# Feed-forward: sums of weight blocks by accumulating DMAs, and fifteen of twenty-two pairs in the seven-product scheme

## The chip, the cores and the metric

The kernel runs on one core of a Trainium2 chip. The metric is device time in microseconds (us) of one execution, the median of several runs; lower is better. The core's engines work side by side and wait for each other through semaphores: TensorE (PE, matrix products; PEld is its weight load), VectorE (DVE), ScalarE (ACT), GpSimd (POOL) and SyncE (SP, which here only issues loads). Sixteen DMA engines carry out the transfers that SP, ACT and POOL issue. Each engine takes its own instructions strictly in program order.

## The reference

The reference computes a two-layer encoder trunk on a sequence of 512 positions of width 1024, in float32. Each layer has a mixer (attention in the first, a chunkwise recurrent mLSTM in the second), a memory cross-attention and a gated convolutional feed-forward part, each behind an RMS norm. Only the feed-forward part is touched:

```python
def conv_ffn(xn, w_up, conv_w, conv_b, w_down):
    h = causal_depthwise_conv(xn @ w_up, conv_w) + conv_b      # w_up: 1024 x 5632
    g, u = jnp.split(h, 2, axis=-1)
    return (jax.nn.gelu(g) * u) @ w_down                       # w_down: 2816 x 1024
```

The width 2816 of `g` and `u` is 22 blocks of 128 columns. A "pair" p is block p of `g` together with block p of `u`; it needs two column blocks of `w_up`, p and 22 + p, each 1024 x 128.

## The kernel before

**Precision by splitting.** Every float32 operand is split in a high part (a cast on ACT) and a low part (a subtraction on DVE, L259), and a product is three matmuls: high by high, low by high, high by low (`mm3`, L268 to L270). Weights arrive as `raw` tiles and are split to `wh` and `wl`.

**A plain pair** (`plain`, L1282). For each of the two column blocks: one load of 512 KB, a split of 128x1024, and 8 x 3 matmuls with 512 columns moving (all positions). DVE then scales the result from PSUM to a tile `hs` (L1291).

**A seven-product pair** (`seven`, L1301). The pair's weights are seen as a 2 x 2 block matrix: row halves of 512 of the model width by the two column blocks, and the activations as 2 x 2 blocks by the same row halves and by halves of 256 positions. Seven block products instead of eight give the result (a scheme of the Strassen-Winograd kind). Each product is 4 x 3 matmuls with 256 columns moving, so the pair has 84 of them, half as wide as the 48 of a plain pair. The price is sums of blocks. With A11 and A12 the halves of `up[p]`, and A21 and A22 those of `up[22 + p]`, as they are stored, four sums are needed: S1 = A21 + A22, S2 = S1 + A11, S3 = A21 + A11, S4 = S2 + A12. Before, DVE makes them, each a TENSOR_TENSOR of 128x512 (`sum4`, L1329), in one tile `sum` with a single buffer; five splits follow (L1317 for the casts): `f3` of A11 and A12, `s2` of S2, `f1` of S1 and S3, `a22` of A22, `s4` of S4. The sums of activation blocks (`th`, `tl`) are made once per layer by `forms` (L1213). On the result side are five more DVE sums of 128x256 (L1372), one copy and one scaled copy on ACT, and a scaling of `hs` (L1393).

**The tail** of each pair (`tail`, L1237): two filter results on ACT, four filter taps on DVE (L1254), the GELU, the product, and the split of the activation `ah`, `al`.

**The down product** (`down`, L1403) works in chunks of four pairs (the last one of six): for each of eight output blocks a load of 256 KB, a split of 128x512, and 12 wide matmuls. These blocks are put between parts of later pairs: `plain` calls `fill` twice and `seven` three times, and each call takes one waiting down block. Eight are put on the list at pairs 5, 9, 13 and 18.

**What sets the order.** The feed-forward part is not written in its final order. Each step is a task with an engine, an estimated duration, what it depends on, a due time and the buffers it takes and frees; `Sched` (L139) plays all engines forward when the kernel is built and gives each engine a fixed order: whatever can start earliest, and of equals the one due first. Buffers are taken in the order in which the tasks were written. `load` (L1142, its DMA at L1145) is a task of SP. At most three `raw` tiles, three split weights of 128x1024 (`h`), two `hs` tiles and four PSUM accumulators are open at a time.

Before, the pairs 4, 6, 8, 10, 12, 14, 15, 17 and 19 of each layer use seven products. POOL does little: it clears two columns of each new `hs` tile (L1277).

## Time and profile before

| What | Value |
|---|---|
| median of 3 runs | 1513.41 us (1512.3 to 1513.85) |
| time of the profiled execution | 1512.78 us |
| its span, first to last instruction | 1511.0 us, 21313 instructions |
| granted TensorE clock, mean | 0.998 |
| first feed-forward part | about 416 to 774 us |
| second feed-forward part | about 1147 us to the end |
| HBM read and written | 143.04 MB and 2.10 MB, 96 GB/s over the span |
| DVE, low part of a 128x1024 weight (L259) | 197 times, 1222 ns |
| DVE, sums of weight blocks (L1329) | 72 times, 685 ns |
| ACT, high part of a 128x1024 weight (L262, L1159, L1317) | 1045 to 1051 ns |
| load of 512 KB / 256 KB / 384 KB, issue to landing | 3.3 / 2.6 / 3.0 us |

The span is one execution recorded by the profiler; the device time is a little longer than the span. Busy times are sums of records, so an engine's share is an average over stages with different limits. Matmuls and DVE operations are pipelined: the record of one runs on while the next has begun, so the distance between two starts is what an operation costs its engine, and the duration in a row is longer than that. "Idle before, releaser" names what an engine had waited for.

### The profile page before, as it was taken

Reading aid. Unit: us, or ns where it says so; the run is one execution under the profiler, and the core shown is the slowest. Engines: PE = TensorE matmul, PEld = TensorE weight load, DVE = VectorE, ACT = ScalarE, POOL = GpSimd, SP = SyncE. Lnnn points to the kernel's source line nnn. Section 1 sums busy time; section 2 is a strip of 40 time slices with the busy share of each in tenths; the row PEclk is TensorE's granted clock in tenths of the full one; section 3 lists DMA queues with packets and bytes.
Section 4 is the critical chain, followed back from the end, with each engine's and each line's share of the span. In section 5 each row is a group of like instructions: output and inputs, shape, how many; then the busy total and the mean of one; then the engine's idle time right before and its main releaser. Section 6 shows DMA issues by size and latency. Waiting matters only on the chain.

```text
span 1511.0 us, 21313 instructions
## 1 busy us (share of the span) xinstructions
PE 1500.0 (99%) x8026; PEld 1281.7 (85%) x8026; DVE 1160.1 (77%) x2155; ACT 774.8 (51%) x1282; POOL 44.0 (3%) x118
## 2 busy tenths in 40 slices
PE   9999999999999999999999999999999999999998
PEld 8888888888888888988888778888888888888887
DVE  7889885766699788897678857666557988889864
ACT  6768564444465444454446634444445554444444
POOL 2000120000000000000001100000000000000000
PEclk9999999999999999999999999999999999999999
DMA  5222233323223333232222222332323332333322
GB/s 179 84 71 84 84 103 108 112 96 100 95 101 100 97 108 109 84 112 88 81 90 84 80 89 93 99 101 99 111 84 109 108 94 95 98 103 106 102 60 77
DMA packets 47480, 146.52 MB, mean 97 GB/s; under 512 B 5649, under 2 KB 5649, under 8 KB 47377
## 3 DMA queue, kind: packets, MB, share of 16 engines
q1 hardware_dynamic: 46368, 144.04, 29.4%
q8 instruction: 63, 1.03, 0.3%
q10 hardware_dynamic: 1008, 1.12, 0.2%
q14 instruction: 41, 0.33, 0.1%
HBM read 143.04 MB, written 2.10 MB: 96 GB/s over the span
## 4 chain that ended last, share of the span: by engine, by line
PE 92%; DVE 3%; ACT 2%; issue 1%; DMA 1%; POOL 0%; SPq 0%; DVEq 0%; POOLq 0%; ACTq 0%
PE acc L268 19%; PE acc L269 19%; PE acc L270 19%; PE w L269 5%; PE w L268 5%; PE w L270 5%; PE acc L330 2%; PE acc L331 2%; PE acc L329 2%; PE s L268 2%; PE s L269 2%; PE s L270 2%; PE w L1595 1%; PE w L681 1%; PE s L395 1%
## 5 line engine op out<-in xcount | busy, mean ns | idle before, releaser
L268 PE MATMUL acc<-xh,wh 128*128 128x512 f32 (+1 forms) x944 | 356.9, 378 | 0.0
L270 PE MATMUL acc<-xh,wl 128*128 128x512 f32 (+1 forms) x944 | 352.8, 374 | 0.0
L269 PE MATMUL acc<-xl,wh 128*128 128x512 f32 (+1 forms) x944 | 352.6, 374 | 0.0
L259 DVE TENSOR_TENSOR wl<-raw,wh 128x1024 fp32r<-128x1024 f32 (+2 forms) x215 | 258.0, 1200 | 51.9 <-ACT wh L262 38.1
L262 ACT CAST wh<-raw 128x1024 fp32r<-128x1024 f32 (+2 forms) x137 | 140.9, 1030 | 168.5 <-PE acc L269 99.6
L270 PEld LDWEIGHTS acc<-xh,wl 128*128 128x128 f32 x944 | 177.5, 188 | 31.7
L268 PEld LDWEIGHTS acc<-xh,wh 128*128 128x128 f32 x944 | 177.6, 188 | 30.4
L269 PEld LDWEIGHTS acc<-xl,wh 128*128 128x128 f32 x944 | 177.7, 188 | 30.3
L1254 DVE SCALAR_TENSOR_TENSOR c<-hs,vec,c 128x512 f32<-128x512 f32 x176 | 128.4, 746 | 7.4 <-ACT c L1247 6.8
L269 PE MATMUL w<-al,wh 128*128 128x512 f32 x304 | 118.5, 390 | 0.0
L268 PE MATMUL w<-ah,wh 128*128 128x512 f32 x304 | 118.5, 390 | 0.0
L270 PE MATMUL w<-ah,wl 128*128 128x512 f32 x304 | 118.3, 389 | 0.0
L1159 ACT CAST wh<-raw 128x1024 fp32r<-128x1024 f32 (+1 forms) x60 | 61.3, 1022 | 77.8 <-PE acc L269 49.3
L1247 ACT ACTIVATE c<-hs,vec 128x512 f32<-128x512 f32 x88 | 70.0, 812 | 40.2 <-DVE hs L1393 23.5
L495 DVE TENSOR_TENSOR x<-w,x 128x512 f32<-128x512 f32 x72 | 49.5, 687 | 31.9 <-PE w L270 31.6
L270 PEld LDWEIGHTS w<-ah,wl 128*128 128x128 f32 x304 | 57.1, 188 | 12.0
L268 PEld LDWEIGHTS w<-ah,wh 128*128 128x128 f32 x304 | 57.1, 188 | 10.9
L269 PEld LDWEIGHTS w<-al,wh 128*128 128x128 f32 x304 | 57.1, 188 | 10.7
L1159 ACT CAST wh<-dr 128x512 fp32r<-128x512 f32 x64 | 39.7, 620 | 47.9 <-issue 17.4
L1268 ACT CAST ah<-c 128x512 fp32r<-128x512 f32 x44 | 27.3, 620 | 68.9 <-DVE c L1264 68.9
L330 PE MATMUL acc<-wl,xh 128*128 128x256 f32 (+1 forms) x192 | 61.9, 323 | 0.2 <-DVE wl L259 0.2
L329 PE MATMUL acc<-wh,xh 128*128 128x256 f32 (+1 forms) x192 | 61.7, 326 | 0.0
(373 smaller groups left out, 3323.4 us busy)
## 6 DMA issues: line engine op xcount, KB each, us to landing
raw<-in_up_dram SPq DMA_DIRECT2D x88, 512.0 KB, 3.3
dr<-in_down_dram SPq DMA_DIRECT2D x64, 256.0 KB, 2.6
raw<-in_xk_dram SPq DMA_DIRECT2D x16, 512.0 KB, 3.3
raw<-in_wo_dram SPq DMA_DIRECT2D x16, 512.0 KB, 3.2
raw<-in_xq_dram SPq DMA_DIRECT2D x16, 512.0 KB, 3.3
raw<-in_xv_dram SPq DMA_DIRECT2D x16, 512.0 KB, 3.3
raw<-in_xo_dram SPq DMA_DIRECT2D x16, 512.0 KB, 3.3
raw<-in_down_dram SPq DMA_DIRECT2D x16, 384.0 KB, 3.0
```

Of the source, the lines that this page charges most:

```text
L259: self.nc.vector.tensor_tensor(out=lo, in0=v, in1=hi.bitcast(F32), op=ALU.subtract)
L262: self.nc.scalar.copy(hi, v)
L268: mm(out, wh, xh, start=first, stop=False, skip_group_check=parts)
L269: mm(out, wh, xl, start=False, stop=False, skip_group_check=parts)
L270: mm(out, wl, xh, start=False, stop=last, skip_group_check=parts)
L329: mm(ps, xh[k][:, ts], wh[:, ws], start=(k == 0), stop=False)
L330: mm(ps, xh[k][:, ts], wl[:, ws], start=False, stop=False)
L331: mm(ps, xl[k][:, ts], wh[:, ws], start=False, stop=(k == 7))
L495: self.nc.vector.tensor_tensor(out=self.x[m][:], in0=ps[:], in1=self.x[m][:], op=ALU.add)
L1159: nc.scalar.copy(st["wh"][:, :cols], st[tag][:, :cols])
L1247: nc.scalar.activation(st["c_"][:, j, :], hs()[:, j, 2:514], AF.Identity, scale=self.col("cw", (layer * 3 + 2) * 44 + blk), bias=self.col( ...
L1254: nc.vector.scalar_tensor_tensor(out=c, in0=hs()[:, j, n : n + 512], scalar=w, in1=c, op0=ALU.mult, op1=ALU.add)
```

## The change

The change touches the feed-forward part of both layers.

- Pairs 4 to 15 and 17 to 19 of each layer use seven products: 15 instead of 9.
- The four DVE sums of a seven-product pair are gone. A tile `sa` is loaded with A11 and A21 side by side (a plain DMA on SP's queue); then an accumulating DMA, issued on POOL's queue, adds A21 and A22 from memory onto it, which leaves S3 and S1. A tile `sb` is loaded with A11, an accumulating DMA adds S1 from `sa` onto it, which leaves S2; after S2 has been split, a third accumulating DMA adds A12 from memory, which leaves S4. Each of them waits for the transfers before it.
- A11 and A12 are loaded once more as a whole for `f3` (`raw`), and A22 alone into a new tile `ra`. In all four plain loads and three accumulating ones per pair.
- The scheduler counts an accumulating DMA as 0.0029 us per column on POOL and 2.5 us until it has landed; a plain load as 0.0017 us per column and 2.0 us, as before.
- `hs` becomes two fixed tiles that POOL clears once per layer. `forms` uses the tile `sa`, of which there are two, in place of `sum`, of which there was one.
- The space that the program sets aside for the descriptors of POOL's DMAs (`dynamic_dma_scratch_size`) is given as 2048, where nothing was given before.

The diff, cut to its core:

```diff
--- before.py
+++ after.py
@@ -23,7 +23,7 @@
 NPAIR = DFF // P
 CHUNKS = [(0, 4), (4, 4), (8, 4), (12, 4), (16, 6)]
 
-SEVEN = (4, 6, 8, 10, 12, 14, 15, 17, 19)
+SEVEN = (4, 5, 6, 7, 8, 9, 10, 11, 12, 13, 14, 15, 17, 18, 19)
 EPS = 1e-6
 
 X_AT, X_STEP = 2.6, 0.6
@@ -1121,7 +1121,7 @@
 
 
         nc, t = self.nc, self.t
-        sc = Sched(raw=3, h=3, s2=1, s4=1, a22=1, sum=1, hs=2, c=1, dr=2, v=1, u2=1, u3=1, act=10, acc=4, s=2, w=2)
+        sc = Sched(raw=3, h=3, s2=1, s4=1, a22=1, sa=2, sb=2, ra=2, hs=2, c=1, dr=2, v=1, u2=1, u3=1, act=10, acc=4, s=2, w=2)
         add = sc.add
         tt = lambda n: 0.14 + 1.06e-3 * n
         act = lambda n: 0.2 + 0.83e-3 * n
@@ -1139,10 +1139,17 @@
         def joined(deps, prio, free):
             return add("-", 0.0, None, deps, prio, (), free, 0.0)
 
+        RAWS = {"raw": (self.wp, 1024, 3), "dr": (mp, 512, 2), "sa": (mp, 1024, 2), "sb": (mp, 512, 2), "ra": (mp, 512, 2)}
+
+        def raw_tile(st, tag):
+            pool, n, bufs = RAWS[tag]
+            st[tag] = self.til(pool, tag, (P, n), bufs=bufs)
+            return st[tag]
+
         def load(st, tag, src, cols, at):
             def fn():
-                st[tag] = self.til(*((self.wp, "raw", (P, 1024)) if tag == "raw" else (mp, tag, (P, 512))), bufs=3 if tag == "raw" else 2)
-                nc.sync.dma_start(st[tag][:, :cols], src)
+                to = raw_tile(st, tag)[:, :cols]
+                nc.sync.dma_start(to.rearrange("p (a b) -> p a b", a=2) if len(src.shape) == 3 else to, src)
 
             return add("SP", 0.0017 * cols, fn, (), at, [(tag, st)], (), 2.0)
 
@@ -1209,6 +1216,9 @@
         self.pad(mp, 192)
         th, tl = ([mp.tile([P, 1024], F32R, name=f"t{i}{layer}{k}", tag=f"t{i}{k}") for k in range(4)] for i in "hl")
         formed, pads = [], []
+        hs2 = [mp.tile([P, 2, 514], F32, name=f"hs{layer}{i}") for i in range(2)]
+        for h in hs2:
+            nc.gpsimd.memset(h[:, :, 0:2], 0.0)
 
         def forms(k, at):
 
@@ -1216,22 +1226,22 @@
 
             def scaled(j):
                 if j == 0:
-                    st["t"] = self.til(mp, "hs", (P, 2, 514))
+                    st["t"] = hs2[st["_hs"]][:, :, 2:514]
                 nc.scalar.activation(st["t"][:, j, :512], self.x[k + 4 * j][:], AF.Identity, scale=self.col("ffn", layer * 8 + k + 4 * j))
 
             def first():
-                st["r"] = self.til(mp, "sum", (P, 1536), bufs=1)[:, :1024]
+                st["r"] = raw_tile(st, "sa")[:]
                 tt_(out=pair(st["r"][:, :512]), in0=pair(st["t"][:, 0, :512]), in1=st["t"][:, :, 256:512], op=ALU.subtract)
 
             T1, T3, T2, T4 = (slice(256 * i, 256 * i + 256) for i in range(4))
             tt_ = nc.vector.tensor_tensor
             a = add("ACT", ACV, lambda: scaled(0), (), at, [("hs", st)])
             a = add("ACT", ACV, lambda: scaled(1), [a], at)
-            a = add("DVE", tt(512), first, [a], at, [("sum", st)])
+            a = add("DVE", tt(512), first, [a], at, [("sa", st)])
             a = add("DVE", tt(256), lambda: tt_(out=st["r"][:, T2], in0=st["t"][:, 1, 256:512], in1=st["r"][:, T1], op=ALU.add), [a], at)
             a = add("DVE", tt(256), lambda: tt_(out=st["r"][:, T4], in0=st["t"][:, 1, 0:256], in1=st["r"][:, T2], op=ALU.subtract), [a], at, (), [("hs", st)])
             h = add("ACT", act(1024), lambda: nc.scalar.copy(th[k][:], st["r"]), [a], at)
-            formed.append(add("DVE", tt(1024), lambda: self.sub(tl[k][:], st["r"], th[k][:]), [h], at, (), [("sum", st)]))
+            formed.append(add("DVE", tt(1024), lambda: self.sub(tl[k][:], st["r"], th[k][:]), [h], at, (), [("sa", st)]))
 
 
         def tail(p, st, deps, at):
@@ -1273,8 +1283,7 @@
 
         def rows(st, at):
             def fn():
-                st["hs_"] = self.til(mp, "hs", (P, 2, 514))
-                nc.gpsimd.memset(st["hs_"][:, :, 0:2], 0.0)
+                st["hs_"] = hs2[st["_hs"]]
 
             return add("-", 0.0, fn, (), at, [("hs", st)])
 
@@ -1299,12 +1308,23 @@
 
 
         def seven(p, fill):
-            st, r1, r2, f1, f3, s2, s4, a22 = ({} for _ in range(8))
+            st, sa, sb, r2, f1, f3, s2, s4, a22 = ({} for _ in range(9))
             at = clock[0]
-            l1 = load(r1, "raw", t["up"][layer, 22 + p], 1024, at - 16.0)
-            l2 = load(r2, "raw", t["up"][layer, p], 1024, at - 16.0)
-            A21, A22, A11, A12 = (lambda: r1["raw"][:, :512]), (lambda: r1["raw"][:, 512:]), (lambda: r2["raw"][:, :512]), (lambda: r2["raw"][:, 512:])
+            A1, A2 = t["up"][layer, p], t["up"][layer, 22 + p]
             tt_ = nc.vector.tensor_tensor
+            up2 = t["up"][layer].rearrange("(j p) r c -> p r j c", j=2)
+
+
+            def onto(out, src, cols, deps, due):
+                return add("POOL", 0.0029 * cols, lambda: nc.gpsimd.dma_start(out(), src(), accum_op=ALU.add), deps, due, (), (), 2.5)
+
+            SB = lambda: sb["sb"][:]
+            b1 = load(sa, "sa", up2[p][:, :, :512], 1024, at - 20.0)
+            b1 = onto(lambda: sa["sa"][:], lambda: A2, 1024, [b1], at - 16.0)
+            b2 = load(sb, "sb", A1[:, :512], 512, at - 18.0)
+            b2 = onto(SB, lambda: sa["sa"][:, 512:], 512, [b1, b2], at - 9.0)
+            l2 = load(r2, "raw", A1, 1024, at - 10.0)
+            l1 = load(a22, "ra", A2[:, 512:], 512, at - 6.0)
 
             def small(s, tag):
                 if tag == "s4" and not pads:
@@ -1319,27 +1339,13 @@
                 h = add("ACT", act(cols), hi, deps, due - 3.0, take)
                 return add("DVE", tt(cols), lambda: self.sub(s["wl"][:, :cols], raw(), s["wh"][:, :cols]), [h], due - 2.0, (), free)
 
-
-            sums = {}
-            S1, S3, S2, S4 = (lambda i=i: sums["t"][:, 512 * i : 512 * i + 512] for i in (0, 1, 2, 2))
-
-            def sum4(out, a, b):
-                if not sums.get("t"):
-                    sums["t"] = self.til(mp, "sum", (P, 1536), bufs=1)
-                tt_(out=out(), in0=a(), in1=b(), op=ALU.add)
-
-            w3 = split(f3, 1024, [l2], at, lambda: parts(f3), [("h", f3)], lambda: r2["raw"][:])
-            b1 = add("DVE", tt(512), lambda: sum4(S1, A21, A22), [l1], at - 6.0, [("sum", sums)])
-            b2 = add("DVE", tt(512), lambda: sum4(S2, S1, A11), [b1, l2], at - 5.5)
-            b3 = add("DVE", tt(512), lambda: sum4(S3, A21, A11), [b1, l2], at - 5.0)
-            w2 = split(s2, 512, [b2], at, lambda: small(s2, "s2"), [("s2", s2)], S2)
-            b4 = add("DVE", tt(512), lambda: sum4(S4, S2, A12), [w2], at - 1.5)
-            w1 = split(f1, 1024, [b3], at + 1.0, lambda: parts(f1), [("h", f1)], lambda: sums["t"][:, :1024])
-            w22 = split(a22, 512, [l1], at + 4.0, lambda: small(a22, "a22"), [("a22", a22)], A22)
-            w4 = split(s4, 512, [b4], at + 5.0, lambda: small(s4, "s4"), [("s4", s4)], S4)
-            joined([w1, w2, w4], at, [("sum", sums)])
-            joined([b1, b3, w22], at, [("raw", r1)])
-            joined([b2, b3, b4, w3], at, [("raw", r2)])
+            w3 = split(f3, 1024, [l2], at, lambda: parts(f3), [("h", f3)], lambda: r2["raw"][:], [("raw", r2)])
+            w2 = split(s2, 512, [b2], at, lambda: small(s2, "s2"), [("s2", s2)], SB)
+            w1 = split(f1, 1024, [b1], at + 1.0, lambda: parts(f1), [("h", f1)], lambda: sa["sa"][:])
+            b4 = onto(SB, lambda: A1[:, 512:], 512, [w2], at - 1.5)
+            w22 = split(a22, 512, [l1], at + 4.0, lambda: small(a22, "a22"), [("a22", a22)], lambda: a22["ra"][:], [("ra", a22)])
+            w4 = split(s4, 512, [b4], at + 5.0, lambda: small(s4, "s4"), [("s4", s4)], SB, [("sb", sb)])
+            joined([w1, b2], at, [("sa", sa)])
 
             def product(s, c, xh, xl, bank, first):
 
@@ -1359,7 +1365,7 @@
             n = 1.42
             p1 = pe(n, lambda: opened("X", bx, "acc", f3, 0, *X(0, 0), "X", True), [w3], [("acc", bx)])
             p6 = pe(n, lambda: opened("Y", by, "acc", s2, 0, *T2, "Y", True), [w2, *formed], [("acc", by)], [("s2", s2)])
-            p5 = pe(n, lambda: opened("R", br, "s", f1, 0, *T1, "R", True), [w1], [("s", br)])
+            p5 = pe(n, lambda: opened("R", br, "s", f1, 512, *T1, "R", True), [w1], [("s", br)])
             get = rows(st, at + 2.0)
 
             def v_():
@@ -1379,7 +1385,7 @@
             p2 = pe(n, lambda: product(f3, 512, *X(1, 0), "X", False), [p1, v], (), [("h", f3)])
             c11 = add("ACT", act(256), lambda: nc.scalar.copy(hs(0, 0)(), bank("X")()), [p2, get], clock[0] + 2.0, (), [("acc", bx)])
             fill()
-            p7 = pe(n, lambda: product(f1, 512, *T3, "Y", False), [u2, p5], (), [("h", f1)])
+            p7 = pe(n, lambda: product(f1, 0, *T3, "Y", False), [u2, p5], (), [("h", f1)])
             u3 = add("DVE", 0.42, lambda: sum_("u3", tmp("u3"), bank("Y"), tmp("v_"), ALU.add), [p7], clock[0], [("u3", bu3)])
             c22 = add("DVE", 0.42, lambda: sum_(None, hs(1, 1), tmp("u3"), bank("R"), ALU.subtract), [u3, p5, get], clock[0], (), [("u3", bu3)])
             fill()
@@ -1793,7 +1799,7 @@
     import concourse.bacc as _bacc
     from concourse.bass_utils import run_bass_kernel_spmd as _run
 
-    nc = _bacc.Bacc("TRN2", target_bir_lowering=False, num_devices=1)
+    nc = _bacc.Bacc("TRN2", target_bir_lowering=False, num_devices=1, dynamic_dma_scratch_size=2048)
     arrays, t = {}, {}
     for name, a in layout(inputs).items():
         arrays[f"in_{name}_dram"] = a
```

## The prediction

> **What bounds the kernel now.** I read the busy line of the page first, then the stretches of the first feed-forward (FF) block (420 to 775 us; the second repeats it from 1151 us), the list of what TensorE (PE) waited for, and the instructions in order of time on PE and VectorE (DVE).
>
> ```profile
> PE 1500.0 (99%) x8026; PEld 1281.7 (85%) x8026; DVE 1160.1 (77%) x2155; ACT 774.8 (51%) x1282; POOL 44.0 (3%) x118
> q1 hardware_dynamic: 46368, 144.04, 29.4%
> ```
>
> ```profile
> 420.00:480.00 60.00, 60.00 (x310) 51.45 (x310) 57.56 (x98) 36.34 (x50) 0.52 (x5) 1.00 0.30 101
> 480.00:680.00 200.00, 200.00 (x1167) 177.17 (x1166) 173.33 (x258) 94.59 (x139) 1.34 (x13) 1.00 0.32 101
> ```
>
> In the second fence the columns are stretch, length, then PE, weight load, DVE, ACT and POOL busy, granted clock, DMA share, GB/s. PE is busy all 200 of 200 us; the longest PE wait in the whole list is 1.3 us, ahead of the attention stages, and none lies in these stretches. DVE is next. A full DVE does not by itself stop PE: in 420 to 480 us it is busy 57.56 of 60 us and PE still loses nothing.
>
> A full PE is not PE at a fixed cost, so I take the distance between starts, not the durations (matmuls overlap). This is one seven-product pair; one row opens each group of 12 matmuls:
>
> ```profile
> 585.22 0.28 PE L268 MATMUL acc<-xh,wh 128*128 128x256 f32 x1
> ...
> 586.65 0.29 PE L268 MATMUL acc<-th,s2h 128*128 128x256 f32 x1
> ...
> 588.03 0.28 PE L268 MATMUL s<-th,wh 128*128 128x256 f32 x1
> ...
> 589.39 0.28 PE L268 MATMUL acc<-xh,wh 128*128 128x256 f32 x1
> ...
> 590.81 0.40 PE L268 MATMUL w<-ah,wh 128*128 128x512 f32 x1
> ...
> 593.56 0.28 PE L268 MATMUL acc<-th,wh 128*128 128x256 f32 x1
> ...
> 594.97 0.39 PE L268 MATMUL acc<-xh,wh 128*128 128x512 f32 x1
> ...
> 597.69 0.28 PE L268 MATMUL acc<-th,a22h 128*128 128x256 f32 x1
> ...
> 599.11 0.28 PE L268 MATMUL s<-xh,s4h 128*128 128x256 f32 x1
> ...
> 600.52 0.39 PE L268 MATMUL acc<-xh,wh 128*128 128x512 f32 x1
> ```
>
> The seven products take 1.43, 1.38, 1.36, 1.42, 1.41, 1.42 and 1.41 us: **9.83 us**. The group at 594.97, half a plain block of the next pair, is 12 wide matmuls in 2.72 us, 0.2267 us each. A plain pair is 48 of these: **10.88 us**.
>
> **The change, part by part.** *More seven-product pairs.* The list goes from 9 to 15 pairs in each of two layers: 12 pairs swapped. Each saves 10.88 - 9.83 = 1.05 us of PE, together **12.6 us**. As PE has no idle time in these stretches, all of it counts if the operands arrive.
>
> *Block sums leave DVE.* Four additions of 128x512 per seven-product pair go; each new one adds other work. These are DVE rows of the first such pair:
>
> ```profile
> 470.24 1.22 DVE L259 TENSOR_TENSOR wl<-raw,wh 128x1024 fp32r<-128x1024 f32 x1
> 471.38 0.68 DVE L259 TENSOR_TENSOR al<-c,ah 128x512 fp32r<-128x512 f32 x1
> 471.98 0.69 DVE L1329 TENSOR_TENSOR sum<-sum,raw 128x512 f32<-128x512 f32 x1
> 472.58 0.68 DVE L1329 TENSOR_TENSOR sum<-raw,raw 128x512 f32<-128x512 f32 x1
> 473.19 0.42 DVE L1372 TENSOR_TENSOR hs<-acc,v 128x256 f32<-128x256 f32 x1
> 473.52 0.68 DVE L259 TENSOR_TENSOR a22l<-raw,a22h 128x512 fp32r<-128x512 f32 x1
> ...
> 478.10 2.74 DVE L1254 SCALAR_TENSOR_TENSOR c<-hs,vec,c 128x512 f32<-128x512 f32 x4
> 480.76 0.69 DVE L495 TENSOR_TENSOR x<-w,x 128x512 f32<-128x512 f32 x1
> ```
>
> From start to start, a 1024-wide operation costs 1.14, a 512-wide one 0.60, a 256-wide one 0.33, and four filter taps 2.66 us. A seven-product pair after the change: splits 2 x 1.14 + 3 x 0.60, five 256-wide sums 1.65, the scaling 1.14, taps 2.66, product and split of the tail 1.20: 10.73 us, where it was 13.13 with the four sums. A down block costs 1.20. Pairs 5 to 8 are all seven-product and share eight down blocks: DVE 4 x 10.73 + 8 x 1.20 = 52.5 us against PE 4 x 9.83 + 8 x 2.72 = 61.1 us, 86%. Before, two of the four were plain (7.34 us DVE each): 50.5 of 63.2 us, 80%. DVE stays below PE, so I cost it at nothing; without that cover each pair of 10.73 us with no down block beside it would run 0.9 us over PE, which a neighbour with three (18.0 us of PE, 14.3 of DVE) pays back. ACT gets some 7.6 us per pair and stays near 60%.
>
> *Loads.* A seven-product pair now moves 512 + 256 + 512 + 256 KB by plain DMA on SP's queue (it was 2 x 512) and 512 + 256 + 256 KB by accumulating DMA on POOL's queue. SP issues four DMAs in place of two, 0.33 us each. Four such pairs and eight down blocks of 256 KB make 8192 KB plain and 4096 KB accumulating. The page's queue moved 144.04 MB in 29.4% of 1511 us, that is 324 GB/s of busy time, so the plain part is 25.9 us. No accumulating DMA is in this trace. From below, it runs like a plain one: 12.9 us, sum 38.8 of 61.1 us, 64%. From above I take twice that, because each byte is read in two places and written once: 25.9 us, sum 51.8 us, 85%. I take the upper one; at either the transfers hide behind PE, and the cover ends at 2.7 times a plain copy ((61.1 - 25.9)/12.9).
> [...]
>
> *Landing.* A 512 KB load lands 3.3 us after issue, 256 KB 2.6 us (page, part 6). The chain of a pair is load, add, second add, ACT cast 0.62, DVE split 0.60: 3.3 + 3.3 + 2.6 + 1.2 = 10.4 us at plain landings, 16 us with the adds at double. The two buffers are released about two pairs ahead of need (some 25 to 30 us, as 9.83 us plus 0 to 8.2 us of down blocks make one pair), so it is hidden. The last add waits for the split of the sum before it and holds POOL's queue meanwhile: behind it stand only the next pairs' adds. The clearing of `hs` leaves that queue (0.10 us each, on no path).
>
> *New gaps.* Pairs 8 and 12 get no down block and are now followed by a seven-product pair. Between products p7 and p4 PE waits for a 0.42 us DVE sum unless something stands between; the row at 594.97 shows a plain half block doing so. What is left is a 1.43 us product of the next pair. Per place nothing to 0.84 us (two sums), four places, 0 to 3.4 us; I take 0.3 each, **1.2 us**, nearer to the first pair of the trace without down blocks, which shows no gap. Elsewhere a queue in better order could gain nothing, PE being full.
>
> **Sum.** Profiled execution: span 1511.0, time 1512.78, so 1.8 us lie around the span. 1511.0 - 12.6 + 1.2 + 1.8 = 1501.4; the median of the runs is 0.6 above the profiled time: **1502.0 us**. 0.2%, about what a measurement of this kernel can tell, is 3 us: below 1510.4 is faster, above 1516.4 slower.
>
> **Rivals.**
> *Late adds in pairs without down blocks.* Pairs 4, 8, 12 and 17 give the last add only five products, 7.0 us, between the start of p6 and that of p3, and cast and split take 1.2 of it. If the add, queued behind 512 KB transfers, lands after 6.6 us instead of 2.6 to 5.2, each place costs 0.8 us, eight places 6 us: **1507 us**. For it: POOL works in order and the DMA share doubles. Against: the split that frees this add can run right after the previous pair's p6, a pair earlier.
>
> *DMA becomes the bound (slower).* If an accumulating byte costs three times a plain one, a group of four needs 25.9 + 38.8 = 64.7 us against 61.1; 30 pairs are 7.5 groups, 27 us: 1500.8 + 27 = **1528 us**. It eats up the gain from 2.86 times on (12.6/7.5 = 1.7 us per group). For it: the DMA share in these stretches is 0.32 and would rise beyond 0.6 even at the plain rate; issue by POOL and its smaller descriptor store are untried here. Against: twice is what the bytes ask for.
>
> *It does not do what it says:* the number of products is in the order of PE's work, which is fixed, so the 12.6 us leave PE in any case; only waits can cover it, and these are the two above.
>
> **How the numbers follow.** Forecast 0.64 (1499 to 1504.5: gaps of 0 to 3.4 us and scatter), late adds 0.18 (1504.5 to 1514, most of it below 1510.4), DMA bound 0.18 (from 1514 on, nearly all above 1516.4). Faster 0.64 + 0.14 = 0.78, same 0.05, slower 0.17. The range 1499 to 1514 holds the first two, 0.82.
>
> **What would show it.** Right: in the FF stretches PE busy throughout with more 256-wide rows (+1008), DVE sums on L1329 gone, DVE near 86%, DMA share 0.55 to 0.75. Late adds: PE waiting for the split of s4 in pairs 4, 8, 12, 17. DMA bound: DMA share above 0.85, PE waiting for s2 or f1 in every pair, and landing times of 10 us and more. I am wrong outright if accumulating DMAs take over 2.7 times a plain one, or if POOL needs more than about 5 us to issue each (three per 15.3 us).

## The result and the profile after

The changed kernel takes 1540.42 us (median of 4 runs, 1539.63 to 1540.91), the kernel before 1513.01 us in the same comparison: a ratio of 1.018, 95% interval 1.0163 to 1.0198. It is 27.4 us slower; I had forecast 1502.0. The profiled execution has a span of 1539.1 us (before 1511.0) and a mean granted clock of 0.990 (before 0.998).

Three lines of the page after: busy time by engine, and the two queues with packets, MB and the time of their packets as a share of 16 engines' span.

```profile
PE 1501.5 (98%) x8458; PEld 1301.7 (85%) x8458; DVE 1156.7 (75%) x2167; ACT 798.6 (52%) x1342; POOL 117.3 (8%) x168
q1 hardware_dynamic: 58848, 159.77, 31.4%
q0 software_dynamic: 12960, 31.46, 12.2%
```

The new line is q0, the accumulating DMAs: 31.46 MB in 12.2% of 1539.1 us is 168 GB/s of busy time, the plain queue's 159.77 MB in 31.4% is 331 GB/s. An accumulating byte took 1.97 times the time of a plain one. Now the two stretches that the prediction showed (stretch, length, PE, weight load, DVE, ACT and POOL busy, granted clock, DMA share, GB/s):

```profile
420.00:480.00 60.00, 55.04 (x279) 46.91 (x278) 48.26 (x82) 32.23 (x44) 7.04 (x8) 0.95 0.63 168
480.00:680.00 200.00, 193.85 (x1311) 179.33 (x1311) 167.92 (x257) 102.01 (x159) 29.74 (x34) 0.99 0.75 191
```

PE, busy throughout before, has holes, although DVE is busy for only 84% of the second stretch and the DMA engines, up from 0.32, for 0.75 of it. What PE waited for (us in total, times, longest):

```profile
PE acc L268 <- ACT v L1373: 14.9, 5, 4.8
PE s L268 <- ACT wh L1337: 9.1, 2, 4.6
```

Seven waits make 24.0 us, and none of them is a DMA wait by name. The longer sum names `v`, a copy of 0.38 us out of an accumulator. To see why a copy is late, take pair 9 and put the rows of three engines side by side. PE (start, duration, row, and in brackets the idle time and its releaser):

```profile
545.46 0.28 PE L270 MATMUL s<-th,wl 128*128 128x256 f32 x1
549.20 0.58 PE L268 MATMUL acc<-xh,wh 128*128 128x256 f32 x1 [3.46 <-ACT v L1373]
549.58 0.42 PE L269 MATMUL acc<-xl,wh 128*128 128x256 f32 x1
```

ACT in the same microseconds:

```profile
539.47 0.61 ACT L1278 CAST ah<-c 128x512 fp32r<-128x512 f32 x1
547.05 0.62 ACT L1337 CAST s2h<-sb 128x512 fp32r<-128x512 f32 x1 [6.97 <-DMA sb<-sa]
547.58 0.61 ACT L1337 CAST a22h<-ra 128x512 fp32r<-128x512 f32 x1
548.76 0.38 ACT L1373 ACTIVATE v<-acc 128x256 f32<-128x256 f32 x1 [0.57 <-DVE hs L1378]
```

And DVE:

```profile
547.70 0.69 DVE L259 TENSOR_TENSOR s2l<-sb,s2h 128x512 fp32r<-128x512 f32 x1 [5.29 <-ACT s2h L1337]
548.31 0.42 DVE L1378 TENSOR_TENSOR hs<-acc,v 128x256 f32<-128x256 f32 x1
```

The cast at 547.05 belongs to **pair 10**: the split of its S2. Both queues stand still for 5 to 7 us until the add `sb<-sa` has landed. Behind it on DVE is the sum at 548.31, of pair 8, that gives up the only `v` buffer, behind it on ACT the `v` of pair 9, and for that PE waits 3.46 us. PE itself takes S2 of pair 10 only at 566.16, 19 us after it landed. So the data were not late for PE; they were late for their place in two in-order queues.

The wait is not all that it costs. Stretches around this gap and around one of 2.14 us (stretch, length, PE busy, granted clock, DMA share, GB/s):

```profile
545.60:549.20 3.60, 0.14 (x3) 1.00 0.65 153
549.20:552.00 2.80, 2.80 (x13) 0.50 0.53 87
612.80:614.90 2.10, 0.22 (x2) 1.00 1.09 287
614.90:617.00 2.10, 1.99 (x14) 1.00 0.70 162
```

After the gap of 3.6 us the granted clock is 0.50 over the 2.8 us shown (from the matmul at 549.58 us on, the starts are 0.21 us apart where 0.118 was usual); after the gap of 2.1 us it stays at 1.00. (The DMA share of 1.09 means that the times of packets overlap there.)

I add up, over both feed-forward blocks, every distance between matmul starts that exceeds the usual 0.2267 or 0.118 us: **gaps** where the excess is over 0.4 us, **slow steps** below that (in the changed kernel some 10 us of them lie in stretches at a clock of 0.50). After: gaps 28.0 us, slow steps 14.3 us, of which 1.2 us were there before. 1511.0 - 12.6 + 28.0 + 13.1 = 1539.5, against a span of 1539.1. Of the gaps 12.0 us lie at pairs 4 and 5 (the first with the scheme), 16.0 at pairs 9 and 13, the ones after the pairs without down blocks (0.6 of it at the end of pair 12).

At pairs 4 and 5 another split stands in front, that of S4 of pair 4. Its add is issued on POOL at 463.83 us and lands 6.6 us later. Behind it on ACT stands the split of S1 and S3 of pair 5, and for that PE waits 4.50 us:

```profile
470.44 0.62 ACT L1337 CAST s4h<-sb 128x512 fp32r<-128x512 f32 x1 [4.47 <-DMA sb<-in_up_dram]
475.14 0.58 PE L268 MATMUL s<-th,wh 128*128 128x256 f32 x1 [4.50 <-ACT wh L1337]
```

### The profile page after: what moved, and what is told of

Read it like the earlier page. It is cut to its first block, busy times and chain, and to the rows that moved or that the text cites. A ratio compares the mean times of both kernels' runs of the same rounds, so it can differ in the third digit from the quotient of the medians.

```text
span 1539.1 us, 22626 instructions
## 1 busy us (share of the span) xinstructions
PE 1501.5 (98%) x8458; PEld 1301.7 (85%) x8458; DVE 1156.7 (75%) x2167; ACT 798.6 (52%) x1342; POOL 117.3 (8%) x168
## 3 DMA queue, kind: packets, MB, share of 16 engines
q1 hardware_dynamic: 58848, 159.77, 31.4%
q0 software_dynamic: 12960, 31.46, 12.2%
## 5 line engine op out<-in xcount | busy, mean ns | idle before, releaser
L268 PE MATMUL acc<-xh,wh 128*128 128x512 f32 (+1 forms) x848 | 311.5, 367 | 14.9 <-ACT v L1373 14.9
L270 PE MATMUL acc<-xh,wl 128*128 128x512 f32 (+1 forms) x848 | 306.7, 362 | 0.0
L269 PE MATMUL acc<-xl,wh 128*128 128x512 f32 (+1 forms) x848 | 306.5, 361 | 0.0
L259 DVE TENSOR_TENSOR wl<-raw,wh 128x1024 fp32r<-128x1024 f32 (+2 forms) x203 | 243.6, 1200 | 42.7 <-ACT wh L262 38.1
L268 PEld LDWEIGHTS acc<-xh,wh 128*128 128x128 f32 x848 | 161.2, 190 | 39.4 <-ACT v L1373 16.1
L270 PEld LDWEIGHTS acc<-xh,wl 128*128 128x128 f32 x848 | 161.4, 190 | 24.1
L269 PEld LDWEIGHTS acc<-xl,wh 128*128 128x128 f32 x848 | 161.5, 190 | 23.2
L1264 DVE SCALAR_TENSOR_TENSOR c<-hs,vec,c 128x512 f32<-128x512 f32 x176 | 127.0, 747 | 11.3 <-ACT c L1257 10.7
L331 PE MATMUL acc<-wh,xl 128*128 128x256 f32 (+1 forms) x192 | 61.7, 322 | 0.0
L268 PE MATMUL acc<-mem,wh 128*128 128x256 f32 (+1 forms) x192 | 61.5, 320 | 0.0
L269 PE MATMUL acc<-mem,wh 128*128 128x256 f32 (+1 forms) x192 | 61.1, 318 | 0.0
```

The costliest lines, as they stand in the source:

```text
L259: self.nc.vector.tensor_tensor(out=lo, in0=v, in1=hi.bitcast(F32), op=ALU.subtract)
L268: mm(out, wh, xh, start=first, stop=False, skip_group_check=parts)
L269: mm(out, wh, xl, start=False, stop=False, skip_group_check=parts)
L270: mm(out, wl, xh, start=False, stop=last, skip_group_check=parts)
L331: mm(ps, xl[k][:, ts], wh[:, ws], start=False, stop=(k == 7))
L1264: nc.vector.scalar_tensor_tensor(out=c, in0=hs()[:, j, n : n + 512], scalar=w, in1=c, op0=ALU.mult, op1=ALU.add)
```

## The experiments

All spans are read with the same sum, 1511.0 less 1.05 us for each swapped pair, plus gaps, plus slow steps less 1.2. "At 8 to 13" is the part of the gaps that lies in pairs 8, 9, 12 and 13, in both blocks. Gaps, slow steps and spans are of the profiled execution, medians of all runs; in e4, e5, e13 and e14 the median lies 2.5 to 3.5 us above the time of the profiled execution.

| kernel | pairs | median us | ratio, 95% interval | gaps | at 8 to 13 | slow steps | sum | span |
|---|---|---|---|---|---|---|---|---|
| changed | 15 | 1540.42 | 1.018 [1.0163, 1.0198] | 28.0 | 16.0 | 14.3 | 1539.5 | 1539.1 |
| e1 nine pairs | 9 | 1528.02 | 1.0094 [1.0079, 1.0109] | 10.0 | none | 6.7 | 1526.5 | 1527.7 |
| e2 vector sums | 15 | 1507.37 | 0.9959 [0.9945, 0.9973] | 3.0 | 3.0 | 6.0 | 1506.2 | 1505.5 |
| e3 later landing | 15 | 1547.92 | 1.0213 [1.0189, 1.0237] | 31.1 | 17.3 | 17.0 | 1545.3 | 1546.8 |
| e4 no add | 15 | 1511.32 | 0.9982 [0.9972, 0.9992] | 6.2 | none | 3.7 | 1507.1 | 1507.0 |
| e5 no 8, 12 | 13 | 1527.33 | 1.0092 [1.0077, 1.0107] | 11.8 | none | 7.4 | 1520.6 | 1522.5 |
| e11 two adds on DVE | 15 | 1516.88 | 1.003 [1.002, 1.0041] | 11.4 | 2.3 | 6.0 | 1514.6 | 1514.8 |
| e12 S2 on DVE | 15 | 1534.26 | 1.0141 [1.0124, 1.0158] | 23.8 | 9.9 | 9.6 | 1530.6 | 1532.4 |
| e13 S4 on DVE | 15 | 1526.08 | 1.009 [1.0066, 1.0113] | 14.4 | 3.1 | 9.5 | 1521.1 | 1520.8 |
| e14 three sa | 15 | 1530.30 | 1.0121 [1.0091, 1.0151] | 18.0 | none | 10.3 | 1525.5 | 1525.7 |
| e15 behind v | 15 | 1536.73 | 1.0152 [1.0135, 1.0169] | 25.9 | 11.3 | 12.9 | 1536.0 | 1536.0 |
| e16 both | 15 | 1530.36 | 1.011 [1.009, 1.013] | 21.4 | 4.3 | 9.2 | 1527.8 | 1529.3 |
| e17 three sa, from 6 | 13 | 1507.14 | 0.9963 [0.9952, 0.9974] | 1.4 | none | 2.6 | 1505.4 | 1505.4 |
| e18 vector, from 6 | 13 | 1505.60 | 0.9949 [0.9932, 0.9966] | 0.0 | none | 2.5 | 1503.9 | 1503.7 |
| e19 S4 on DVE, from 6 | 13 | 1506.08 | 0.995 [0.9935, 0.9965] | 0.7 | none | 1.7 | 1503.8 | 1504.0 |

The sum meets each span of the table within 2 us, over a width of 43 us. So each of these experiments can be read as one question: where do the gaps come from? In the first expectations theory A is the one above, work that waits for adds put ahead of ready work in in-order queues; theory B is that the accumulating DMAs are too slow whatever the order.

**Pairs and sums apart (e1, e2).** e1 is the changed kernel with the old list of nine pairs, e2 the kernel before with the new list of fifteen:

```diff
-SEVEN = (4, 5, 6, 7, 8, 9, 10, 11, 12, 13, 14, 15, 17, 18, 19)
+SEVEN = (4, 6, 8, 10, 12, 14, 15, 17, 19)
```

> The changed kernel with the old list of nine seven-product pairs, so that only the adding DMAs are left of the change. Theory A (fixed order: ACT meets a split of a sum that a late adding DMA still has to deliver, while the instruction that PE needs stands behind it; it bites where two seven-product pairs follow each other with few down blocks): plain pairs stand between, the gaps at pairs 9 and 13 are gone, at most the one at the start of the run of seven-product pairs is left; 1513 to 1522 us. Theory B (an adding DMA is so dear that the transfers are the bound): 18 pairs with adds instead of 30, so about 18/30 of the 28 plus 12.6 us lost by the changed kernel, 25 us over before: about 1538 us.

> The kernel before with the new list of fifteen pairs, the sums still made by DVE. PE has 12.6 us less to do. DVE needs 4 x 13.13 + 9.6 = 62.1 us per group of four such pairs against 61.1 us of PE, and one tile for the sums serves all pairs. If DVE only just becomes the bound: 1503 to 1513 us. If the single tile for the sums and the waits between the engines cost more than that: above 1513, up to 1540 us. Neither theory on the adding DMAs bears on it; it says whether more pairs could be had without them.

The loss sits in the adds, the gain in the pairs. e1, with no more products saved than before, loses 14 us by its first pairs alone, more than A allowed and less than B. e2 is faster than the kernel before, with DVE busy for 198.13 of 200 us and PE still for 198.61:

```profile
480.00:680.00 200.00, 198.61 (x1362) 183.01 (x1361) 198.13 (x317) 107.34 (x166) 1.44 (x14) 1.00 0.34 102
```

**The planner's numbers and the order (e3, e6, e9).** e3 gives the planner longer landings (loads 3.4 for 2.0, adds 5.0 for 2.5 us, both on top of the bytes); e6 makes the program keep the planner's order on all engines, e9 on ACT and DVE alone:

```diff
-        sc.run()
+        with self.tc.manual_schedule():
+            sc.run()
```

> The changed kernel with two numbers of its planner changed: a plain load is taken to land 3.4 us after issue's end instead of 2.0, an adding DMA 5.0 instead of 2.5. The same instructions in another order. Theory A: ACT no longer meets splits before their data, the gaps of 3.5 to 5 us go, and with them the half clock behind each; 1502 to 1510 us. Theory B: the order does not matter, since the transfers are late in any order; 1530 to 1545 us.

> The changed kernel, with every engine of the feed-forward part held to the order in which the kernel's planner emits the instructions. In the changed kernel the framework that builds the program orders them a second time and lets one pass another that it takes to be ready sooner: at pair 9 of each layer the program has ACT split the sum S2 of pair 10 ahead of the copy v of pair 9, where the planner had v first. Theory A (such an order, with a split in front that waits for an adding DMA): the gaps of 2 to 5 us in pairs 9 and 13 go (16 us in the two layers, and some 7 us of half clock behind them), those at the first two seven-product pairs stay: 1514 to 1524 us. Theory B (the adds land too late for any order): 1535 to 1545 us.

> As the run that holds every engine to the planner's order, but only ACT and DVE are held to it; PE, SP and POOL are ordered by the framework as in the changed kernel. Theory A: the blocking is on ACT and DVE, so this gives the same as holding all five, 1514 to 1524 us. Theory B: 1535 to 1545 us. If it is the order of PE, POOL or SP that matters: no change from 1540 us here, and a change in the other run.

e3 came out slower than the change in three of its four runs (the fourth took 1540.18 us): pair 10's S2 split waits 7.7 us at the head of ACT, as before. In e6 (1556.16 us, ratio 1.0287 [1.027, 1.0304]) the gaps at pairs 9 and 13 fall from 16.0 to 6.8 us. Held to the planner's order, ACT makes `v` of pair 9 at 555.02 us and the split of pair 10's S2 behind it, at 560.95. So the order that the planner gives is not the last word: the framework that builds the program orders it a second time, and there the split got ahead of `v`. That this is why e3 cured nothing is likely, but not shown. In exchange gaps of 2.8 us come up elsewhere in e6, and PE is idle for much of the start of each feed-forward part (stretch, length, PE busy, granted clock, DMA share, GB/s):

```profile
415.00:434.00 19.00, 10.71 (x33) 0.66 0.15 45
```

At 1168 to 1187 us it is 10.71 us again, while the changed kernel has PE busy for 19.00 us from 412 to 431 us. e9 (1550.13, 1.0251 [1.0226, 1.0275]) is like it, with 10.75 us at the start. By their times none of the three fits A, and all three lie above B's range as well. Order matters, but A with order alone as the cure falls.

**The add alone (e4).** The three accumulating DMAs of a pair become plain copies at the same places; the additions are left out.

```diff
-nc.gpsimd.dma_start(out(), src(), accum_op=ALU.add)
+nc.gpsimd.dma_start(out(), src())
```

> The changed kernel in the same order, with the adding DMAs issued by POOL as plain copies onto the same tiles (the additions of the weight blocks are left out). Theory A: the order is the same, the copies land 1 to 2 us sooner, so the waits on ACT shorten or go: 1502 to 1525 us. Theory B: the price of the second read is gone, the DMA share in the middle of the feed-forward part falls from 0.75 to about 0.6, and the time goes to about 1502 us. Both expect it faster; what tells is whether gaps are left at the same places (A) with a DMA share that is no bound.

The order of the instructions is the same on every engine, and the same bytes go through the same queue, in 6.3% for 12.2% of the span:

```profile
q0 software_dynamic: 9120, 31.46, 6.3%
```

Pair 10's S2 split now waits 1.87 us on ACT where it was 6.97, and PE has no gap beyond pairs 4 and 5:

```profile
536.28 0.62 ACT L1337 CAST s2h<-sb 128x512 fp32r<-128x512 f32 x1 [1.87 <-DMA sb<-sa]
```

So it takes both: the add's doubled time, and a split that stands in the queue when its data are not there.

**Room for the forms (e8, e10).** The forms of the activations hold the `sa` buffers until 448.9 and 456.0 us. e8 builds them in a `raw` tile, e10 does that in the planner's order.

```diff
-                st["r"] = raw_tile(st, "sa")[:]
+                st["r"] = raw_tile(st, "raw")[:]
```

> The changed kernel, with the sums of activation blocks made in a raw tile in place of an sa tile, so that the loads and adds of the first two seven-product pairs need not wait until these sums are done (in the changed kernel the first add is issued at 453 us, 8 us before PE reaches pair 4). The order is the framework's as before. Theory A and B both have the gaps at pairs 4 and 5 go: 12 us and some 6 us of half clock, 1540 - 18 = 1522 us, with those at pairs 9 and 13 still there. If the first pairs are late for another reason (adds that land in 6 us and more whenever transfers crowd): little change, 1535 to 1542 us.

> Both edits: every engine in the planner's order, and the sums of activation blocks in a raw tile. Theory A: no long gap is left, PE has its 12.6 us less: 1500 to 1506 us. Theory B: the adds are late in pairs 9 and 13 still: 1515 to 1525 us.

Both miss: 1577.83 us (1.0426 [1.0411, 1.0442]) and 1587.33 (1.0489 [1.0473, 1.0504]). The edit takes `raw` buffers from the plain loads, and in e8 each block has two gaps of some 11.1 and 8.3 us at plain pairs. The gaps at pairs 4 and 5 were gone, but with PE that far behind this shows little.

**Which add (e11, e12, e13).** S2, S4 or both are summed by DVE again; the large add stays. In all three the load of `raw` also moves up, to the place of the load of `sb` or ahead of it.

```diff
-b2 = onto(SB, lambda: sa["sa"][:, 512:], 512, [b1, b2], at - 9.0)
+b2 = add("DVE", tt(512), sum2, [b1, l2], at - 6.0, [("sb", sb)])
...
-b4 = onto(SB, lambda: A1[:, 512:], 512, [w2], at - 1.5)
+b4 = add("DVE", tt(512), lambda: tt_(out=SB(), in0=SB(), in1=r2["raw"][:, 512:], op=ALU.add), [w2, l2], at - 1.5)
```

> The changed kernel with its 15 pairs and its large accumulating DMA of 512 KB (S1 and S3 of a pair) kept, but S2 and S4 summed by VectorE again: S2 from the second half of the large sum and the first half of the raw block, S4 in place from S2 and the second half of the raw block. So the load of 256 KB into the small buffer and the two accumulating DMAs of 256 KB are gone, and VectorE has 8 sums of 0.685 us more in a group of four pairs: 52.5 + 5.5 = 58.0 of 61.1 us. Theory 'splits that wait for the small adds at the head of ACT's and VectorE's queues' expects the gaps at pairs 9 and 13 (16.0 us over both layers) to go, 1502 to 1512 us, less than before (1513). The rival, that the large add with its 5.7 us and the ring of sa buffers is the trouble, expects the gaps to stay: 1530 us or more.

> The changed kernel with only S2 summed by VectorE (4 x 0.685 us more in a group of four pairs, 55.2 of 61.1), the large add and the last add of 256 KB (S4, from memory) left on the DMA queue. Theory 'it is the add of the large sum's half into the small buffer (6.5 us at pair 9, with S2's split of the next pair waiting for it on ACT ahead of v)' expects the gaps at pairs 9 and 13 to go or to fall below 4 us in sum, 1505 to 1518 us. If the last add is at fault as well, since S4's split stood 1.1 us on ACT behind it, half of the 16 us stays: 1520 to 1530. If the DMA queue's adds as such are the cause, however few, 1530 or more.

> The counterpart: only S4 summed by VectorE (55.2 of 61.1 us again), S2 made by load and accumulating DMA as in the changed kernel. Theory of the add into the small buffer expects the gaps at pairs 9 and 13 to stay about as they are (16 us in sum), 1530 to 1542 us. If the last add is at fault, 1505 to 1518.

I had named the wrong one of the two: without S2's add (e12) 9.9 us stay at pairs 8 to 13, without S4's (e13) 3.1. In e12 another instruction blocks. DVE, in order of time:

```profile
538.10 0.69 DVE L1328 TENSOR_TENSOR sb<-sa,raw 128x512 f32<-128x512 f32 x1 [1.22 <-DMA sa<-in_up_dram]
538.71 0.74 DVE L1264 SCALAR_TENSOR_TENSOR c<-hs,vec,c 128x512 f32<-128x512 f32 x1
539.37 1.22 DVE L259 TENSOR_TENSOR wl<-sa,wh 128x1024 fp32r<-128x1024 f32 x1
540.51 0.41 DVE L1383 TENSOR_TENSOR u<-acc,v 128x256 f32<-128x256 f32 x1
```

The sum of pair 10's S2 now waits itself for the large add, and `u3` of pair 8 stands behind it and two more; PE waits for that `u3` 1.5 us, ahead of p4. e11 has the same sum and one wait less: 2.3 us there, but 9.1 us of gaps elsewhere, its start among them, and 4.8 us more of slow steps keep it above the kernel before. For DVE's load there is only the estimate in its expectation, 58.0 of 61.1 us for four pairs. So giving up S4's add helps most at these places, but e12 shows that a sum on DVE can take over the blocking: in both kernels what waited first for the late transfer held up its queue (6.97 us on ACT in the changed kernel, 1.22 us on DVE here).

**The short pairs and the buffers (e5, e14).** e5 takes pairs 8 and 12, which have no down block between their products, out of the list. e14 has three `sa` buffers.

```diff
-        sc = Sched(raw=3, h=3, s2=1, s4=1, a22=1, sa=2, sb=2, ...
+        sc = Sched(raw=3, h=3, s2=1, s4=1, a22=1, sa=3, sb=2, ...
```

> The changed kernel with pairs 8 and 12 (those without down blocks between their products) in the plain scheme again, 13 of 22 pairs. If the stalls at pairs 9 and 13 come from the short seven-product pair ahead of them (8 or 12: no down blocks, so the next pair's chain of load, add and add has some 10.9 us where it needs 18), the gaps of 16.0 us and their slow steps of some 7 us go, against 4 x 1.05 us lost by the scheme: 1540.4 - 23 + 4.2, so 1518 to 1526 us. If any run of seven-product pairs stalls, 1535 or more.

> The changed kernel with three buffers for the large sum (sa) in place of two, nothing else changed in the text. In the changed kernel the load for pair 10's large sum starts only when pair 8's split has freed its buffer (528.97 us), and load, add and second add then take 18.1 us, to 547.05. Theory 'the buffer comes free too late': with a third buffer the load starts a pair earlier (10.9 us or more), the chain is done before ACT comes to S2's split, and the gaps at pairs 9 and 13 (16.0 us over both layers, with some 7 us of half clock) go: 1514 to 1522 us; the gaps at the start, where the forms hold two of the buffers, may shrink as well: down to 1508. Rival 'the adds' own time and the order in ACT's queue': earlier buffers change nothing, since the planner puts the split earlier again; 1535 or more.

Each of the two takes all of the 16.0 us away; e5 misses its number by a little more than a us, e14 by 8. In e5 the DMA share from 480 to 680 us is still 0.71 and PE is busy 200.00 of 200.00 us, so the rate of the DMAs is not the bound: theory B falls. In e14 the load of pair 10's large sum is issued at 518.13 us, in the changed kernel at 528.97, though e14's PE is some 5 us behind there; S2's split waits 2.25 us in place of 6.97. PE alone, in e14 (columns as above):

```profile
474.10:481.20 7.10, 0.19 (x2) 0.68 0.66 129
540.00:560.00 20.00, 20.00 (x152) 1.00 0.95 199
```

The second line is pair 9's place, without a hole. The first says why e14 missed its number: at pair 4 the gap grew to 7.1 us. Two large adds are issued there at 465.51 and 468.89, S4's add at 466.05 lands among them only at some 475 us, and ACT and DVE stand behind its split.

**The order of one split (e15, e16).** With two and with three buffers, S2's cast is fixed behind the `v` of the pair before, and its subtraction behind that pair's `u2`.

```diff
-                    nc.scalar.copy(s2["wh"][:], SB())
+                    with self.tc.issue_after(back["vi"]()):
+                        nc.scalar.copy(s2["wh"][:], SB())
```

> The changed kernel with only the order changed: on ACT the cast of S2 of a pair is put behind the copy v of the pair before it, and on VectorE the subtraction of S2's split behind that pair's u2 (both for the planner and as a fixed order). The buffers and DMAs are as they were, so the data land as late as before. Theory 'data late at the head of an in-order queue, not late for TensorE': S2 of pair 10 lands at 547.05 and TensorE asks for it some 8 us later, so with v ahead of the cast the gaps at pairs 9 and 13 (16.0 us) go; 1514 to 1524 us. If the data are really late for TensorE, the gap moves to the product with S2 and its size stays: 1535 or more.

> Both: three sa buffers and the fixed place of S2's split. If buffer and order are two ways out of the same stall, no more than the better of the two is gained, 1510 to 1522 us; what is left are the gaps at the first seven-product pairs (12.0 us over both layers with their half clock). If the planner's other choices stall instead, 1525 to 1540. Without any gap the scheme's 12 pairs would give some 1500 us.

`v` of pair 9 comes at 542.39 in e15, in time. But now S4's split of pair 9, which waits for the last add, heads DVE's queue, and PE's next product waits 1.91 us for the `u2` behind it:

```profile
549.63 0.69 DVE L259 TENSOR_TENSOR s4l<-sb,s4h 128x512 fp32r<-128x512 f32 x1 [4.66 <-ACT s4h L1337]
550.24 0.42 DVE L1405 TENSOR_TENSOR u<-acc,v 128x256 f32<-128x256 f32 x1
```

11.3 of 16.0 us stay. By the number this was to mean that PE lacks the data; the rows say otherwise, since it is S4's split that blocks and not S2 that is missed. Here moving one waiting instruction handed the stall to the next (4.66 us on DVE), and fixing this order on top of three buffers (e16) gained nothing: 1530.36 us against e14's 1530.30.

**The start, and whether the adds pay at all (e17, e18, e19).** Three `sa` buffers, with pairs 4 and 5 plain (e17); the same 13 pairs with the sums on DVE in the kernel before (e18); e17 with S4 on DVE (e19).

```diff
-SEVEN = (4, 5, 6, 7, 8, 9, 10, 11, 12, 13, 14, 15, 17, 18, 19)
+SEVEN = (6, 7, 8, 9, 10, 11, 12, 13, 14, 15, 17, 18, 19)
```

> The changed kernel with three sa buffers, and pairs 4 and 5 in the plain scheme: 13 of 22 pairs, 4 more than in the kernel before, so 4 x 2 x 1.05 = 8.4 us to be saved. Theory 'the stalls at the first seven-product pairs come from the adds' late start (the forms of the activations hold the sa buffers until about 454 us and the plain loads fill the queue)': two pairs later, at some 490 us, the first chains are done in time; no gap over 2 us is left and the time is 1503 to 1509 us, less than before (1513). Rival 'the first two pairs with adds stall wherever they stand': gaps of 7 to 9 us in each layer stay, 1520 us or more.

> The kernel before with its sums on VectorE and the same 13 pairs (6 to 15 and 17 to 19), for comparison with the last: what the accumulating DMAs themselves bring or cost. VectorE was busy for 198.1 of 200 us in the middle of the feed-forward with 15 pairs. 13 pairs save 8.4 us, and some stalls of VectorE's stay: 1505 to 1512 us, within 3 us of the run with 15 pairs (1507.4). If the accumulating version of the same pairs is faster than this, relieving VectorE was worth something once the chains were in time.

> The same 13 pairs and three sa buffers, with only the last add (S4) given back to VectorE, so that two adds a pair are left on the DMA queue. If a chain of three adds is in time once the buffers are three and the start is later, this is within 2 us of the version with all three adds; if S4's add is late at the head of ACT's queue even then, this one is faster by 2 us or more: 1500 to 1506.

All three are as expected; they are 0.4 to 0.5% faster than the kernel before. Two pairs later the adds cost PE only 1.4 us of gaps, though in e17 ACT still stands 6.08 us, until 473.81, for S4's add of the first such pair: the plain pairs leave PE work meanwhile. So the start gaps came from the late start, not from being first. e17 and e18 from 480 to 680 us, in this order:

```profile
480.00:680.00 200.00, 198.82 (x1350) 183.28 (x1349) 174.65 (x264) 105.74 (x165) 27.91 (x32) 1.00 0.72 181
```

```profile
480.00:680.00 200.00, 199.94 (x1356) 184.54 (x1355) 192.13 (x303) 103.67 (x161) 1.33 (x13) 1.00 0.32 99
```

Moving the sums takes 17.5 us off DVE and buys nothing: with DVE 96% busy PE still has its 199.94 us. Between the three ratios the intervals overlap; I don't rank them.

## Why the prediction was wrong

- **Products: right.** 1.05 us per swapped pair. e18 swaps 8, and its span falls by 7.3 us with 1.3 us more of slow steps: 8.6, where 8.4 was worked out.
- **DVE: right.** 84% of 480 to 680 us after (87% in e17, with PE nearly full), at no cost to PE by itself. What I did not draw from it: if DVE is no bound, relieving it is worth nothing, as e17 and e18 show (17.5 us off DVE in 200 us, and no gain).
- **Loads: right at the upper end.** 1.97 times a plain byte (1.98 in e4's comparison: 12.2% of 1539.1 us against 6.3% of 1507.0) where I took 2, and a share of 0.75, at the top of the 0.55 to 0.75 I named. The 2 was my estimate from the bytes, which no run had shown by then; that the second read is the cause is not shown either, only that the same bytes without the addition go at the plain rate (e4: 31.46 MB in 6.3% of 1507.0 us is 331 GB/s). The rival "DMA becomes the bound" did not come about: its price of three was not reached, and e5 runs PE without a hole at a share of 0.71. Its time, 1528, was nearer than my forecast by luck: the chance of 0.17 for a slower kernel rested on this rival, and the time came out slower for a reason that none of the rivals names in full.
- **Landing: the step that failed.** "The two buffers are released about two pairs ahead of need (some 25 to 30 us ...), so it is hidden." The chain was the smaller error: load, add and second add took 18.1 us at pair 10 (528.97 to 547.05), where my terms for these three, 3.3 + 6.6 + 5.2, make 15.1 (the 16 holds cast and split as well), and 25 us would have covered both. The larger error was the need: I took PE's, and PE indeed takes S2 only 37 us after the release. But the split stands on ACT where the framework put it, ahead of `v` of pair 9, and ACT came to it at 540.08, 11.1 us after the release; 7.0 us were missing. What I wrote of POOL's queue ("behind it stand only the next pairs' adds") I should have asked of ACT's and DVE's, where everything else of a pair stands behind.
- **Late adds in pairs without down blocks: the place nearly, the size not.** Pairs 8 and 12 are the cause (e5), and it shows a pair later, by the split of S2 of the pair after that. The landing that this rival feared did come: the last add takes 6.5 us in the median, where it had 6.6. I priced 6 us, what PE would wait for the data itself; it was 15.4 us, and half clock behind it.
- **The start: not in the prediction.** I looked at pairs in the middle. At pairs 4 and 5 the buffers are held by the forms and the queue is full of loads (DMA share 0.63 over 420 to 480 us), which makes 12.0 us. Pair 4 is on the list of the rival of late adds, and S4's add is late there; but it blocks ACT's queue, and PE waits for another split.
- **Half clock: not in the sum.** The gaps brought 13.1 us more of slow steps with them, some 10 of these at half clock.
- **New gaps: right.** Ahead of p4 in pairs 8 and 12 one of the four places shows a gap, 0.63 us behind the matmul at 607.74; I took 0.3 for each.

What stays open: why the framework puts S2's split ahead of `v`, and whether fifteen pairs with adds could beat e2 in an order without these stalls.

## What to carry to other kernels

Compare a transfer's landing with the moment when the in-order queue comes to the first instruction that waits for it, not with the moment when the busiest engine needs the data (here, at pair 10, a landing at 547.05 us against 540.08, when ACT came to the split, and 566.16, when PE took it); then ask what ready work stands behind that instruction. Moving work off an engine that was not the bound gained nothing here by itself (17.5 us off DVE from e18 to e17); try the other half of a change without it (here e2: the pairs alone were 6 us faster than before). Where a bound engine stalls, add what it loses after the stall (here 13.1 us of slow steps beside 28.0 us of gaps).

## What the runs showed of the hardware

Around each of the five gaps of 3.6 to 5.0 us of the changed kernel the granted clock of TensorE falls to 0.50, and stays there for 3.4 us (549.2 to 552.6, 1293.3 to 1296.7 and 1361.6 to 1365.0 us) or 6.8 us (474.1 to 480.9 and 1218.2 to 1225.0); after the gap of 2.1 us it is 1.00. The runs show no shortest gap for this. In e1 a gap of 2.75 us, ended by the matmul at 1218.49 us, leaves the clock at 1.00 up to 1224 us. In e14 one of 1.98 us, ended at 464.96, is followed by half clock, though only 1.5 us later (columns as for the gaps above):

```profile
466.50:469.80 3.30, 3.30 (x18) 0.50 0.97 200
```

Why half clock follows the gap of 1.98 us in e14 and not the one of 2.75 us in e1, and what sets the lengths of 3.4 and 6.8 us, stays open.

An accumulating DMA of 512 KB landed 5.7 us after its issue in the changed kernel (median), the plain copy in its place in e4 4.4 us. The one of 256 KB inside SBUF took 4.3 us in the median and 6.5 us at pair 10, as a copy 2.4 us at both; the one of 256 KB from memory 6.5 and 3.3 us (medians). It also took POOL longer to issue: 0.86 us in the median of the changed kernel's 90, against 0.53 to 0.55 for the copies of e4 from 505 to 545 us.
